# A delta-rule head's decay matrix kept in device memory between its two uses

## The chip, the cores and the metric

One Trainium2 chip, of which one core runs the kernel: a TensorE (PE, with its weight loads listed apart as PEld), a VectorE (DVE), a ScalarE (ACT), a GpSimd (POOL) and a SyncE (SP) that only issues transfers. The metric is the time of one launch on the device in microseconds, taken outside the profiler; it was 1414.25 us in the median of three runs (1413.27, 1414.25 and 1415.5). A profile is one further execution, with every instruction's start and duration.

## The reference

One layer of a hybrid block, for one sequence of 512 tokens and a model width of 1024, in 32-bit floats. The normed input is projected to twelve groups of columns. Branch A is a gated delta rule with 8 heads (keys and queries 128 wide, values 256 wide), branch B a retention with 4 heads; the two are gated, added, projected, and an MLP of width 4096 follows. For branch A the lines that matter here are these:

```python
decay = jnp.exp(jnp.where(causal, g_cum[..., :, None] - g_cum[..., None, :], -jnp.inf))
lower = jnp.where(strict, jnp.einsum('bhncd,bhnmd->bhncm', k_beta, k) * decay, 0.0)
t_inv = lax.linalg.triangular_solve(lower, eye, left_side=True, lower=True, unit_diagonal=True)
attn = jnp.where(causal, jnp.einsum('bhncd,bhnmd->bhncm', q, k) * decay, 0.0)
```

The matrix `decay` depends on the gates alone, is the same in both products, and is used twice for each head: once with the keys alone, to make the triangular matrix that is inverted, and once with queries and keys, to make the weights inside a chunk. The kernel works in chunks of 128 tokens, so a head has four such matrices of 128 by 128.

## The kernel before

The kernel is one program without loops at run time. A scheduler arranges it: each instruction goes to the queue of its engine in an order that the scheduler chooses from the order of the source, from priorities and from its own estimate of times, and each queue then runs strictly in that order. An instruction that waits holds up all behind it in its queue. Tiles with one tag share one buffer or a few (`bufs`): the next tile under the tag can be written only when every reader of the last one is done.

Most of the time goes into products with weights (lines 81 to 83: each product of exact halves is three matmuls of 512 columns). SP loads the weights in pieces of 512 KB, ACT rounds a piece to its high half (`whi`, L100) and DVE subtracts to get the low half (`wlo`, L101).

Branch A runs in this order of the source (lines 657 to 677): `keys(0)` for heads 0 to 3, `base_inverse(0)`, `values_queries(0)` for heads 0 and 1, `keys(1)` for heads 4 to 7, `double_blocks`, and then four rounds, each with the `recurrence` of two heads, the `values_queries` of the next two, the gating (`gated`) and a product with a branch weight. The parts overlap freely in time.

`decays(h, pool)` makes the four decay matrices of a head: for the two halves of the gate's logarithm, ACT scales a triangle of ones four times into `tg` (L390, eight instructions a head), PE multiplies each `tg` with a strict triangle into PSUM (L391, two matmuls a head) and ACT takes the exponential into `dt` (L393). It is called from `keys` (L438) and from `values_queries` (L555).

`dt` has one buffer, as the tag is given without `bufs`. In `keys`, eight DVE instructions read it for a head (L445 writes `mt`, which lives in `acc`; L448 scales `kd`), in `values_queries` four (L561 writes `at`, which POOL then masks at L565). `double_blocks` puts its own scratch `y` under the same tag (L505, written at L511 and L527, read by matmuls at L515, L518 and L530). So exponentials, these products and `y` take turns in one buffer.

POOL issues the transfers of the inverse through device memory from its own queue: `mt` out in four pieces (L458), back as one block to a partition (`mb`, L464), the finished inverses out (L481, L482) and back (`rt` L485, `rn` L495). Between them stand small memsets for the convolution (L357) and the mask (L565). The inverse itself is 31 steps of two DVE instructions (L473, L479). PSUM tiles under the tag `dl` have three banks, shared by decays, key products, inverses and recurrences.

Of the kernel before, what the change touches and what calls it, by code (L numbers as in the profile page):

```python
# [19 lines left out]
P = 128  # L20
# [40 lines left out]
def hybrid_block_kernel(ctx: ExitStack, tc: tile.TileContext, a: dict, out: bass.AP):  # L61
# [23 lines left out]
    def weights(src, k0, nk, c0, ncols, keep=None):  # L85
        """nk blocks of 128 rows, ncols columns, in exact halves; split ahead of other work that is due."""
        n = nk * ncols
        i = next(loads)
        raw = raw_pools[i % len(raw_pools)].tile([P, 1024], F32, tag="raw", name="raw", bufs=2)
        nc.sync.dma_start(  # L90
            raw[:, :n].rearrange("p (k c) -> p k c", k=nk),
            src[k0 * P : (k0 + nk) * P, c0 : c0 + ncols].rearrange("(k p) c -> p k c", p=P),
        )
        if keep is None:
            hi = ring.tile([P, 1024], F32R, tag="whi", name="whi")
            lo = ring.tile([P, 1024], F32R, tag="wlo", name="wlo")
        else:
            hi, lo = keep
        with tc.high_priority(200 if i >= 6 else 0):
            nc.scalar.copy(hi[:, :n], raw[:, :n])  # L100
            nc.vector.tensor_tensor(lo[:, :n], raw[:, :n], hi[:, :n], ALU.subtract)  # L101
        return (
            hi[:, :n].rearrange("p (k c) -> p k c", k=nk),
            lo[:, :n].rearrange("p (k c) -> p k c", k=nk),
        )

    def feature_major(src, xs, c0, ncols, kts, krow0=0):
        """[feature, token] products of ncols columns: PSUM tiles of 128 features."""
        nf = ncols // P
        pss = [psm.tile([P, xs[0].shape[2]], F32, tag="mm", name="mm") for _ in range(nf)]  # L110
        step = 1024 // ncols
        for k0 in range(0, kts, step):
            wh, wl = weights(src, krow0 + k0, step, c0, ncols)
            for f in range(nf):
                fs = slice(f * P, (f + 1) * P)
                for kk in range(step):
                    kt = k0 + kk
                    mm3(
                        pss[f],
                        (wh[:, kk, fs], wl[:, kk, fs]),  # L120
                        (xs[0][:, kt, :], xs[1][:, kt, :]),
                        kt == 0,
                        kt == kts - 1,
                    )
        return pss

    def token_major(src, lhs, c0, kts, krow0=0):
        """[token, 512 columns] products: one PSUM tile for each 128 tokens."""
        pss = [psm.tile([P, T], F32, tag="mm", name="mm") for _ in range(4)]
        for k0 in range(0, kts, 2):  # L130
            wh, wl = weights(src, krow0 + k0, 2, c0, 512)
            for t in range(4):
                tt = slice(t * P, (t + 1) * P)
                for kk in range(2):
                    kt = k0 + kk
                    mm3(
                        pss[t],
                        [x[:, tt] for x in lhs(kt)],
                        (wh[:, kk, :], wl[:, kk, :]),
                        kt == 0,  # L140
                        kt == kts - 1,
                    )
        return pss
# [4 lines left out]
    def rsqrt(xv, n, name):  # L148
        """1/sqrt of a positive [P, n] tile."""
        yi = sm.tile([P, n], I32, tag=f"rs_i{n}", name="rs_i")  # L150
# [13 lines left out]

# [1 line left out]
    cmat = cp.tile([P, 3 * P], F32, name="cmat")  # L166
# [13 lines left out]

# [1 line left out]
    xs = [act.tile([P, 8, T], F32R, tag="actT", name="actT") for _ in range(2)]  # L182
# [8 lines left out]
    def root(v):  # L191
        """1/sqrt of a positive [P, n] tile."""
        n = v.shape[1]
# [9 lines left out]
    def rows_to_features(xn, t, dst):  # L203
        """Transposes the [128 tokens, 1024] tile into the halves dst."""
        tt = slice(t * P, (t + 1) * P)
# [9 lines left out]
    with tc.tile_pool(name="xp", bufs=2) as xp:  # L215
# [62 lines left out]

# [1 line left out]
        baT = xp.tile([16, T], F32, tag="baT", name="baT")  # L280
# [44 lines left out]
    def gate_rows(pss, o_t, zt):  # L325
        """o * rstd * silu(z) in place, token-major."""
        for t in range(4):
# [25 lines left out]

# [1 line left out]
    def conv_silu(ps, ch, dst, pool):  # L355
# [28 lines left out]
    def decays(h, pool):  # L384
        """exp(sum of g over (m, c]) for m <= c, else 1: [m, chunk, c]."""
        pd = psx.tile([P, T], F32, tag="dl", name="dl", bufs=3)
# [5 lines left out]
        dt = pool.tile([P, 4, P], F32, tag="dt", name="dt")  # L392
        nc.scalar.activation(dt, pd.rearrange("p (c n) -> p c n", c=4), AF.Exp)  # L393
        return dt

# [9 lines left out]
    with tc.tile_pool(name="pa", bufs=1) as pa:  # L405
# [46 lines left out]
        def base_inverse(g4, pool):  # L452
            """Unit lower triangular inverses of 64 diagonal 32-blocks, one to a partition."""
            scr_m, scr_r, scr_t = (dr.tile([4, 16, 1024], F32, tag=f"scr{i}", name="scr") for i in range(3))
# [33 lines left out]
        def double_blocks(pool, scr_r, m0):  # L488
            """From 32-blocks to the transposed 128-block inverses, for two heads."""
            rn = pool.tile([P, 8, 64], F32, tag="qf", name="rn", bufs=2)  # L490
# [42 lines left out]
        def values_queries(g2, pool):  # L533
# [16 lines left out]
            for hh in range(2):  # L550
# [3 lines left out]
                sum_squares(to_tokens(qf[:, hh, :]), ssq[:, 4 * hh : 4 * hh + 4], junk)  # L554
                dt = decays(h, pool)  # L555
                pk = psx.tile([P, 4, P], F32, tag="dl", name="dl", bufs=3)
# [10 lines left out]
            )  # L567
            # r_q * dk**-0.5
            rq = pool.tile([P, 8], F32, tag="rq", name="rq", bufs=2)
# [4 lines left out]
        def recurrence(g2, vq, pool):  # L574
# [61 lines left out]

            # rstd of the true output r_q * dk**-0.5 * o; a half of it for silu(z)
            v = pool.tile([P, 8], F32, tag="ov", name="ov")
# [40 lines left out]

# [1 line left out]
    with tc.tile_pool(name="pb", bufs=1) as pb_:  # L681
# [129 lines left out]

# [1 line left out]
    with tc.tile_pool(name="pm", bufs=1) as pm:  # L813
# [10 lines left out]
        def row_tiles(src, lhs, krow0, keeps, done):  # L824
            """[token, 1024] products, two tiles of 128 tokens and then one by one; the weights stay on chip."""
            kept = {}
# [27 lines left out]
        def norm_halves(parts):  # L854
            """rstd of rows that come in two halves; what else is done with a half may follow it."""
            ss = sm.tile([P, 2], F32, tag="nh_s", name="nh_s")
# [9 lines left out]
        def add_normed(t, parts, w):  # L866
            """x2[t] += rmsnorm(parts) * w."""
            fw = pm.tile([P, D], F32, tag="ym", name="fw", bufs=2)
# [129 lines left out]
```

## Time and profile before

| | |
|---|---|
| three timed runs | 1413.27, 1414.25, 1415.5 us |
| span of the profiled execution, first to last instruction | 1410.7 us |
| the profiled execution's own time outside the profiler | not listed; the median run is 3.55 us above the span |
| PE busy | 1394.6 us, 99% |
| DVE busy | 809.0 us, 57% |
| ACT busy | 571.7 us, 41% |
| POOL busy | 53.0 us, 4% |
| device memory read and written | 124.93 MB and 3.67 MB |

Busy time is the union of an engine's instructions. PE's instructions overlap in the pipeline, so that a matmul of 512 columns is shown with 0.39 us and the next one starts 0.23 us after it; the chain of waits, which follows the last instruction back to what released it at each step, counts the latter. The granted clock of PE is 0.997 of full speed over the span. All that the change touches lies in the first 390 us.

### The profile page before, as it was taken

To read this page: it belongs to the slowest core of one execution; us is meant where nothing else is said; L and a number is where in the kernel's file an instruction comes from. 1 tells how busy PE (TensorE), PEld (TensorE's weight loads), DVE (VectorE), ACT (ScalarE), POOL (GpSimd) and SP (SyncE) were. 2 spreads that over 40 slices of the span, in tenths; PEclk is the share of its full clock that TensorE was granted. 3 is DMA by queue.
4 is the path that set the end of the run, shared out by engine and by line. 5 is a ranking of instruction groups with operands and counts; after the bars stand their busy time and mean duration, and the time that the engine had idled before them with its cause. 6 is when DMAs were issued, how large, how long until landed. Compare 5 with 4: busy or idle time off the path is not lost.

```text
span 1410.7 us, 17493 instructions
## 1 busy us (share of the span) xinstructions
PE 1394.6 (99%) x6766; PEld 1139.7 (81%) x6766; DVE 809.0 (57%) x1463; ACT 571.7 (41%) x1082; POOL 53.0 (4%) x100
## 2 busy tenths in 40 slices
PE   8999999999999999999999999999999999999997
PEld 6888787878888888888888888888888888888886
DVE  5599889944765564436445455445685333343445
ACT  6778564624534233233342323223464333132331
POOL 1111300200000000000000000000000000000000
PEclk9999999999999999999999999999999999999999
DMA  5232412221221342333223232232724232232321
GB/s 157 75 95 75 114 31 75 73 76 46 89 90 48 103 135 83 97 95 93 75 90 98 75 90 90 75 90 75 238 90 135 90 101 94 92 102 90 108 72 60
DMA packets 69942, 129.74 MB, mean 92 GB/s; under 512 B 4608, under 2 KB 18066, under 8 KB 69859
## 3 DMA queue, kind: packets, MB, share of 16 engines
q1 hardware_dynamic: 66128, 119.03, 26.8%
q0 software_dynamic: 3008, 8.34, 2.1%
q8 instruction: 53, 0.87, 0.3%
q10 hardware_dynamic: 722, 1.25, 0.2%
q14 instruction: 31, 0.25, 0.1%
HBM read 124.93 MB, written 3.67 MB: 91 GB/s over the span
## 4 chain that ended last, share of the span: by engine, by line
PE 92%; DVE 5%; ACT 1%; issue 1%; DMA 1%; SPq 0%; DVEq 0%; ACTq 0%
PE mm L81 27%; PE mm L82 27%; PE mm L83 27%; PE tr L179 2%; DVE c_y L367 1%; PE dl L83 1%; PE dl L82 1%; PE dl L81 1%; PE dl L598 1%; PE dl L626 1%; DVE wlo L101 1%; PE dl L590 1%; PE dl L606 1%; PE dl L619 1%; DVE tmp L473 1%
## 5 line engine op out<-in xcount | busy, mean ns | idle before, releaser
L101 DVE TENSOR_TENSOR wlo<-raw,whi 128x1024 fp32r<-128x1024 f32 x208 | 254.3, 1223 | 387.8 <-ACT whi L100 386.6
L100 ACT CAST whi<-raw 128x1024 fp32r<-128x1024 f32 x208 | 218.3, 1050 | 514.0 <-PE mm L82 282.1
L82 PE MATMUL mm<-actT,whi 128*128 128x512 f32 (+1 forms) x528 | 207.7, 393 | 1.2 <-DVE actT L213 1.2
L81 PE MATMUL mm<-actT,whi 128*128 128x512 f32 (+1 forms) x528 | 206.8, 393 | 1.0 <-ACT actT L212 1.0
L83 PE MATMUL mm<-actT,wlo 128*128 128x512 f32 (+1 forms) x528 | 207.3, 393 | 0.0
L81 PE MATMUL mm<-whi,actT 128*128 128x512 f32 x472 | 185.9, 394 | 0.1
L82 PE MATMUL mm<-wlo,actT 128*128 128x512 f32 x472 | 185.4, 393 | 0.0
L83 PE MATMUL mm<-whi,actT 128*128 128x512 f32 x472 | 185.2, 393 | 0.0
L81 PEld LDWEIGHTS mm<-actT,whi 128*128 128x128 f32 x528 | 99.8, 189 | 21.4 <-ACT actT L212 1.3
L82 PEld LDWEIGHTS mm<-actT,whi 128*128 128x128 f32 x528 | 100.1, 190 | 20.4 <-DVE actT L213 1.4
L83 PEld LDWEIGHTS mm<-actT,wlo 128*128 128x128 f32 x528 | 100.0, 189 | 19.0
L81 PE MATMUL mm<-hn,whi 128*128 128x512 f32 (+1 forms) x288 | 106.3, 370 | 0.6 <-DVE r L921 0.5
L82 PE MATMUL mm<-hn,whi 128*128 128x512 f32 (+1 forms) x288 | 106.2, 369 | 0.0
L83 PE MATMUL mm<-hn,wlo 128*128 128x512 f32 (+1 forms) x288 | 106.0, 369 | 0.0
L81 PEld LDWEIGHTS mm<-whi,actT 128*128 128x128 f32 x472 | 88.6, 188 | 19.0 <-ACT c_y L365 0.5
L83 PEld LDWEIGHTS mm<-whi,actT 128*128 128x128 f32 x472 | 88.6, 188 | 18.2
L82 PEld LDWEIGHTS mm<-wlo,actT 128*128 128x128 f32 x472 | 88.6, 188 | 17.9
L81 PE MATMUL mm<-og,whi 128*128 128x512 f32 x256 | 100.3, 392 | 0.0
L82 PE MATMUL mm<-og,whi 128*128 128x512 f32 x256 | 99.6, 389 | 0.0
L83 PE MATMUL mm<-og,wlo 128*128 128x512 f32 x256 | 98.5, 390 | 0.0
L367 DVE SCALAR_TENSOR_TENSOR c_y<-c_raw,convw,c_y 128x512 f32<-128x512 f32 x96 | 70.5, 752 | 3.4 <-ACT c_y L365 2.8
L81 PEld LDWEIGHTS mm<-hn,whi 128*128 128x128 f32 x288 | 54.0, 187 | 11.4 <-issue 0.7
(286 smaller groups left out, 2077.0 us busy)
## 6 DMA issues: line engine op xcount, KB each, us to landing
raw<-in_w_in_dram SPq DMA_DIRECT2D x113, 512.0 KB, 3.6
raw<-in_w_up_dram SPq DMA_DIRECT2D x36, 512.0 KB, 3.6
raw<-in_w_down_dram SPq DMA_DIRECT2D x32, 512.0 KB, 3.6
raw<-in_w_br_a_dram SPq DMA_DIRECT2D x16, 512.0 KB, 3.6
raw<-in_w_br_b_dram SPq DMA_DIRECT2D x16, 512.0 KB, 3.6
raw<-in_w_out_dram SPq DMA_DIRECT2D x8, 512.0 KB, 3.7
x<-in_x_dram SPq DMA_DIRECT2D x4, 512.0 KB, 6.4
acc<-in_x_dram POOLq DMA_DIRECT2D x4, 512.0 KB, 3.8
```

The lines of the kernel that those rows point to most:

```text
L81: nc.tensor.matmul(ps, lh, rh, start=first, stop=False)
L82: nc.tensor.matmul(ps, lh, rl, start=False, stop=False)
L83: nc.tensor.matmul(ps, ll, rh, start=False, stop=last)
L100: nc.scalar.copy(hi[:, :n], raw[:, :n])
L101: nc.vector.tensor_tensor(lo[:, :n], raw[:, :n], hi[:, :n], ALU.subtract)
L179: nc.tensor.transpose(ps, src, ident)
L367: nc.vector.scalar_tensor_tensor(y, raw[:, j : j + T], tap(j), y, ALU.mult, ALU.add)
L473: nc.vector.tensor_tensor(t3, mb3[:, j, j + 1 : 32].unsqueeze(2).to_broadcast([64, nr, ni]), rb3[:, j, 0:ni].unsqueeze(1).to_broadcast([64 ...
L590: nc.tensor.matmul(ks[:, hh, :], kf[:, h0 + hh, cs], state[:, hh, :], start=True, stop=True)
L598: nc.tensor.matmul(px[:, hh, :], rt[:, nn[hh], :], vx[:, hh, :], start=True, stop=True)
L606: nc.tensor.matmul(pc[:, hh, :], kd[:, nn[hh], :], vn[:, hh, :], start=True, stop=True)
L619: nc.tensor.matmul(qs[:, hh, :], qf[:, hh, cs], prev[:, hh, :], start=True, stop=True)
```

## The change

`decays`, which is now called from `keys` alone, also writes its result to device memory, to a tile of its own for each head, by a transfer that POOL issues. `values_queries` no longer computes the matrices: `decays_again` takes the same kind of tile under the same tag `dt` and fills it by a transfer from device memory, again issued by POOL. What is left out of the diff below is the removal of comments and docstrings.

```diff
     def decays(h, pool):
...
         dt = pool.tile([P, 4, P], F32, tag="dt", name="dt")
         nc.scalar.activation(dt, pd.rearrange("p (c n) -> p c n", c=4), AF.Exp)
+        kept_decays[h] = dr.tile([P, 4, P], F32, tag=f"dt{h}", name="dts", bufs=1)
+        nc.gpsimd.dma_start(kept_decays[h], dt)
+        return dt
+
+    kept_decays = {}
+
+    def decays_again(h, pool):
+        dt = pool.tile([P, 4, P], F32, tag="dt", name="dt")
+        nc.gpsimd.dma_start(dt, kept_decays[h])
         return dt
...
-                dt = decays(h, pool)
+                dt = decays_again(h, pool)
```

## Rows read from the trace of the kernel before

**Rows 1.** Page, block 4: the chain that ended last, by engine.

```profile
PE 92%; DVE 5%; ACT 1%; issue 1%; DMA 1%; SPq 0%; DVEq 0%; ACTq 0%
```

**Rows 2.** Stretches: length, busy of PE, PEld, DVE, ACT, POOL, clock, DMA.

```profile
90.00:147.50 57.50, 56.34 (x278) 45.91 (x276) 56.93 (x146) 43.59 (x122) 8.86 (x12) 1.00 0.28 83
...
205.50:251.00 45.50, 45.29 (x213) 36.35 (x212) 44.81 (x110) 24.63 (x45) 4.65 (x6) 1.00 0.20 60
262.00:290.00 28.00, 27.90 (x237) 22.70 (x235) 19.74 (x58) 16.76 (x54) 5.80 (x11) 1.00 0.21 65
```

**Rows 3.** DVE's waits from 89.5 to 147.5: total us, times, longest.

```profile
DVE c_y L367 <- ACT c_y L365: 0.5, 1, 0.5
DVE wlo L101 <- ACT whi L100: 0.2, 1, 0.2
```

**Rows 4.** DVE's waits from 205.5 to 251.

```profile
DVE at L561 <- PE dl L559: 0.3, 1, 0.3
```

**Rows 5.** PE's weight loads' waits from 118 to 260.

```profile
PEld tr L179 <- DVE c_y L371: 1.0, 1, 1.0
```

**Rows 6.** Chain of waits, decay matmuls for queries: start us, us, what.

```profile
91.17 0.47 PE dl L391 x2
...
204.02 0.67 PE dl L391 x2
...
385.55 0.47 PE dl L391 x2
```

**Rows 7.** Groups by line: busy us, mean ns, idle before.

```profile
L390 ACT ACTIVATE tg<-cmat,ghi 128x128 fp32r<-128x128 f32 x64 | 22.3, 401 | 4.5 <-PE dl L391 3.2 <-DVE ghi L315 1.2
```

**Rows 8.** POOL's transfers of 256 KB from 40 to 450: count, KB, us to landing.

```profile
scr<-mrb POOLq DMA_DIRECT2D x2, 256.0 KB, 2.9
...
scr<-acc POOLq DMA_DIRECT2D x2, 256.0 KB, 3.5
...
mrb<-scr POOLq DMA_DIRECT2D x1, 256.0 KB, 3.3
acc<-scr POOLq DMA_DIRECT2D x1, 256.0 KB, 4.0
```

**Rows 9.** Timeline of ACT, `dt` of heads 5, 6, 7: start us, us.

```profile
149.98 0.60 ACT L393 ACTIVATE dt<-dl 128x512 f32<-128x512 f32 x1 [0.99 <-DVE kd L448]
...
154.06 0.59 ACT L393 ACTIVATE dt<-dl 128x512 f32<-128x512 f32 x1
...
157.57 0.60 ACT L393 ACTIVATE dt<-dl 128x512 f32<-128x512 f32 x1 [0.59 <-DVE kd L448]
```

**Rows 10.** Timeline of POOL at the same time.

```profile
149.56 2.57 POOL L485 DMA_DIRECT2D rt<-scr  x4 [0.43 <-DMA scr<-mrb]
```

**Rows 11.** Timeline of DVE, the next writer of that buffer.

```profile
161.55 0.88 DVE L511 COPY y<-dl 32x256 f32<-32x256 f32 x2
```

**Rows 12.** Timeline of DVE, first products of heads 2 and 3.

```profile
205.69 0.35 DVE L561 SCALAR_TENSOR_TENSOR at<-dl,rk,dt 128x128 f32<-128x128 f32 x1 [0.34 <-PE dl L559]
...
208.65 0.34 DVE L561 SCALAR_TENSOR_TENSOR at<-dl,rk,dt 128x128 f32<-128x128 f32 x1
```

**Rows 13.** Timeline of POOL, the first inverse's way through memory.

```profile
81.12 2.62 POOL L458 DMA_DIRECT2D scr<-acc  x4 [19.59 <-DVE kd L448]
...
88.69 0.55 POOL L464 DMA_DIRECT2D mrb<-scr  x1 [0.53 <-issue]
```

**Rows 14.** Timeline of DVE, first step of that inverse.

```profile
93.71 0.18 DVE L473 TENSOR_TENSOR tmp<-mrb 64x31 f32<-64x31 f32 x1
```

**Rows 15.** Timeline of DVE, products of heads 4 and 5.

```profile
271.50 1.13 DVE L561 SCALAR_TENSOR_TENSOR at<-dl,rk,dt 128x128 f32<-128x128 f32 x4 [0.60 <-PE dl L559]
...
277.12 1.13 DVE L561 SCALAR_TENSOR_TENSOR at<-dl,rk,dt 128x128 f32<-128x128 f32 x4 [0.30 <-ACT dt L393]
```

**Rows 16.** Timeline of POOL, the same store of 256 KB in both inverses.

```profile
144.61 0.55 POOL L481 DMA_DIRECT2D scr<-mrb  x1 [8.75 <-DVE rs_t L156]
...
249.07 1.15 POOL L481 DMA_DIRECT2D scr<-acc  x1 [3.62 <-DVE acc L479]
```

## The prediction

> **What bounds the kernel now.** I read the page first: busy times and the chain of waits. PE is busy for 99% of the span (the table above) and the chain runs through PE for 92% and through DVE for 5% [rows 1]. The reader should take from it that PE time removed can be worth its full length, but that about 70 us of the chain belong to DVE, and that one has to know where. All that is removed lies before 390 us, so the second view is the table of stretches. From 90 to 147.5 us DVE is busy for 56.93 of 57.50 us, and from 205.5 to 251 us for 44.81 of 45.50; from 262 to 290 it is busy for only 19.74 of 28 while PE is full [rows 2]. The list of DVE's waits says the same: two waits of 0.5 and 0.2 us in the first stretch [rows 3], 0.3 us in the second for anything that matters here [rows 4]. At the end of the first stretch PE waits 1.0 us for a DVE instruction of the convolution [rows 5]. So PE and DVE run neck and neck in two stretches, with DVE setting the pace there, and PE alone sets it afterwards. The chain of waits for the decay matmuls of the queries (first, fourth and last of the six pairs that stand as pairs) shows what each costs PE: 0.47 us a head [rows 6]; the 0.67 at 204.02 has 0.20 of other waiting in it. Two heads (3 and 5) have their two matmuls apart; I count them at 0.47 too.
>
> **What goes.** For eight heads: two matmuls, eight scalings on ACT and one exponential. On PE that is 8 x 0.47 = 3.76 us. On ACT it is 8 x (8 x 0.40 + 0.59) = 30 us of instruction time [rows 7, 9], but ACT is busy for only 43.59 of 57.50 us in its fullest of these stretches [rows 2] and off the chain, so I cost it at nothing; if ACT were what holds DVE's splits, at most the 0.2 us of that wait [rows 3] is to be had.
>
> What of the 3.76 us reaches the end is settled by stretch. Heads 0 and 1 (0.94 us) lie from 91 to 105 us, inside the first DVE stretch. DVE has no less to do than before; it can run earlier only by the time it idles after 91 us, 0.2 us; the 0.5 us wait comes before [rows 3]. Bounds 0 and 0.94; I take 0.2. Heads 2 and 3 (0.94 us) stand at the head of the second DVE stretch. DVE idles 0.3 us for the product that follows the matmuls of head 2 [rows 4, 12], which an earlier product would give back, but see the load below: I take 0. Heads 4 to 7 (4 x 0.47 = 1.88 us) lie where PE alone is full [rows 2]: 1.88. Sum: 2.1 us gained.
>
> **What comes: eight stores.** A transfer of 256 KB issued by POOL lands 2.9 to 4.0 us after its issue [rows 8]; for stores 2.9 to 3.5, and I use 3.2. The store reads `dt`, so the next writer of that one buffer now waits for the landing and not only for DVE's eight reads. In `keys(1)`: the matrix of head 5 is there at 149.98 + 0.60 = 150.58 [rows 9]. POOL is then in the middle of four issues of 0.64 us for `rt` [rows 10]; between two of them the store goes out at about 151.0 and lands at 154.2, when the exponential of head 6 started at 154.06: 0.15 late. Then 154.8 + 3.2 = 158.0 against 157.57 for head 7, 0.45 late, and 158.6 + 3.2 = 161.8 against the `y` of `double_blocks` at 161.55 [rows 11], 0.3 late. I take 0.4 us, all of it on PE, whose inverse matmuls read `y`. The low bound is 0 (issue at once, 2.9 us: 153.5, 157.6, 161.1). The high bound has the store behind all four `rt` issues and 3.5 us: 152.1 + 3.5 = 155.6, then 159.7, then 163.8, 2.3 us late. Queued behind a waiting store on POOL are the rest of the `rt` issues and the third `rn`; their readers come after `y` and lose nothing more than it does.
>
> In `keys(0)` the same spacing holds, and heads 2 and 3 could be late by up to the same 2.3 us. That delays the four pieces of `mt` that POOL sends out at 81.12. Their last issue ends at 83.74, and they are fetched back at 88.69 [rows 13]; DVE first uses them at 93.71 [rows 14]. The fetch takes 3.3 us [rows 8], so 1.7 us are spare behind it, and before it 5 us, of which a landing takes at most 4. I cost this at nothing; without that cover it would be up to 2.3 us into a stretch where DVE has none to give.
>
> **Eight loads.** Each waits for the last reader of the buffer; I use the 3.3 us of the load [rows 8]. Head 0's buffer is free at 81.1, when DVE's last read for head 3 lets POOL go on [rows 13], ten us before its use. Head 2's is held by `y` until the matmuls before 204.02 [rows 6] are done: 204.0 + 3.3 = 207.3 against 205.69, 1.6 late. DVE's four products take some 1.4 us among other work, so head 3's load goes out at 208.7 and lands at 212.0 against 208.65 [rows 12], 3.4 late. What is queued behind on DVE is the second inverse, 62 instructions of which two thirds are still to come, and the splits of the weights for PE. The bounds are 0, if the order puts these instructions ahead of the products, and 3.4, if DVE stands. I take 0: among DVE's waits in both stretches no transfer occurs [rows 3, 4], although the inverse's blocks come by transfers of the same size, so the order has been leaving room for them. Head 5's load goes out when head 4's products end at 272.63 and lands at 275.9, before 277.12 [rows 15]: 0. Heads 1 and 7 are late or early by less than 2 us with much other work before their reader: 0. Also, the matmuls of the next parts find a `dl` bank free more often, as the decays took one each; I give it nothing.
>
> The Trainium skill has a rule against this change: by "SBUF — State Buffer", section "SBUF: two separate sides", POOL cannot write the descriptors of its transfers while DVE runs a copy in one of its fast modes. The trace agrees in one place: the same store takes POOL 0.55 us at 144.61 and 1.15 us at 249.07 [rows 16]. By the row at 144.61 an issue costs what the sum has; by the rule each one beside DVE costs up to 0.6 us more. It has a rival below.
>
> **The sum.** 2.1 - 0.4 = 1.7 us gained. The profiled span of 1410.7 becomes 1409.0. Its own time outside the profiler isn't listed; the median run lies 3.55 us above the span, and I let that stand: 1414.25 - 1.7 = 1412.5 us.
>
> **Rivals.**
> 1. PE gets it all: 1414.25 - 3.76 = 1410.5 us. For it speaks the 92% of PE in the chain [rows 1], and that the order of every queue is chosen anew, so that DVE's full stretches may be filled otherwise. Against it: DVE's work there is unchanged.
> 2. The one `dt` buffer becomes the bound, and the kernel gets slower. Each store and each load holds it for more than 3 us, in `keys(1)` up to 2.3 us are lost and in the second DVE stretch 3.4: 1414.25 - 2.1 + 2.3 + 3.4 = 1417.9 us. It decides from the point at which these waits pass 2.1 us together. For it: DVE and PE are both nearly without idle time there [rows 2], so a stall isn't absorbed. Against it: no DVE wait on a transfer stands in these stretches.
> 3. POOL's issue is stretched beside DVE. Five transfers follow one another through the buffer with somebody waiting (stores of heads 5, 6, 7, loads of 2 and 3); at 1.15 - 0.55 = 0.6 us each that is 3.0 us: 1412.5 + 3.0 = 1415.5 us. Against it: only one issue in the trace is stretched like this [rows 16]. The skill's section above would have this case.
> 4. Nothing: the 1.88 us of the last heads too are given back at the next wait for ACT or DVE, 1414.3 us. For it: the gating and the recurrence that follow alternate between the engines. Against it: PE was full there.
>
> **Chances.** The forecast 0.38, with a range of its own from 1411.2 to 1414.0 (bounds 0 to 2.3 us of store wait cut to the likelier half); rival 1 0.22; rival 2 0.24; rival 3 0.08; rival 4 0.08. The range from 1409.8 to 1418.0 leaves out some 0.1 on the side of rival 2 and a little less on that of rival 1. A measurement of this kernel can tell a change from none from about 0.2%, 2.8 us: faster is below 1411.4, slower above 1417.1. Faster gets rival 1 and 0.05 of the forecast, 0.27; slower gets 0.20 of rival 2 and 0.02 of rival 3, 0.22; the rest is 0.51.
>
> **What would show it.** PE's instructions fall by 16 and its busy time by some 4 us. In the chain the DVE share before 251 us stays or grows. The exponentials of heads 6 and 7 name a transfer as what they waited for, by less than 0.5 us. DVE's waits name `dt` for heads 2 and 3, and if that is over 1 us in sum, rival 2 has begun. POOL's issues of the new transfers last 0.55 to 0.65 us; 1 us or more speaks for rival 3. PE's waits from 262 to 392 us stay as they are; if they grow by over 1 us, rival 4. I am wrong altogether if the new order of the queues moves PE's waits elsewhere by more than these sums, which shows as lost time after 400 us.

## The result, and the profile after

The changed kernel took 1420.38 us in the median of six executions against 1413.47 for the kernel before on the same chip: ratio 1.004 (95% interval 1.0029 to 1.0051), so 0.4% slower. Forecast were 1412.5 and a range up to 1418.0. Five of the six lie from 1416.89 to 1421.79 and enter the ratio; the sixth, which is the one that was profiled, had a mean granted clock of 0.754 and a span of 1729.2 us, so everything below is read from another profile of the same kernel, the first experiment, at 0.996. That set took 1418.79 us, ratio 1.0029 (1.0017 to 1.0041).

The line numbers of the changed kernel: stores L395, loads L402, key products L451, `mt` L454, `kd` L457, the inverse L482 and L488, the values' scaling L549, the queries' products L570. First its page: the span, PE, the new transfers with their median landing, and the chain by engine.

```profile
span 1416.5 us, 17422 instructions
...
PE 1393.0 (98%) x6750; PEld 1137.7 (80%) x6750; DVE 807.8 (57%) x1463; ACT 550.3 (39%) x1010; POOL 64.1 (5%) x116
...
PE 88%; DVE 5%; DMA 3%; ACT 2%; issue 1%; POOL 1%; SPq 0%; DVEq 0%; ACTq 0%; POOLq 0%
...
dts<-dt POOLq DMA_DIRECT2D x8, 256.0 KB, 3.2
```

The median landing is the 3.2 us that the prediction took. But in the chain PE has lost 4 points against [rows 1], and transfers and ACT have gained 3. The chain between 71 and 83 us says where: in `keys(0)` it runs exponential, store, exponential, store.

```profile
71.68 0.60 ACT dt L393
...
72.56 4.94 DMA dts<-dt
...
77.61 0.61 ACT dt L393
...
78.50 3.47 DMA dts<-dt
...
82.07 0.61 ACT dt L393
```

The same exponentials on ACT's timeline (start, duration, in brackets the idle time before it and who ended it); in the kernel before none of them waited for a transfer:

```profile
71.68 0.59 ACT L393 ACTIVATE dt<-dl 128x512 f32<-128x512 f32 x1
...
77.61 0.60 ACT L393 ACTIVATE dt<-dl 128x512 f32<-128x512 f32 x1 [2.54 <-DMA dts<-dt]
...
82.07 0.60 ACT L393 ACTIVATE dt<-dl 128x512 f32<-128x512 f32 x1 [1.06 <-DMA dts<-dt]
...
156.45 0.60 ACT L393 ACTIVATE dt<-dl 128x512 f32<-128x512 f32 x1 [1.72 <-DMA dts<-dt]
```

ACT's own idle time would cost nothing by itself. But the key products of the same head need a bank of PSUM under the tag `dl`. In PE's queue the decay matmuls of the next head stand ahead of these products (at 74.89), and the bank that the products take is the one that the exponential of their own head empties, so they wait for it. PE's queue is in order, so the weight products behind them wait too. PE's timeline:

```profile
75.59 0.39 PE L81 MATMUL mm<-actT,whi 128*128 128x512 f32 x1
78.26 0.94 PE L451 MATMUL dl<-kf 128*128 128x128 f32 x6 [2.29 <-ACT dt L393]
```

The first matmul starts at 75.59 and its successor should follow 0.23 us later; it follows at 78.26. That is the largest single loss, 2.4 us.

The waits of the whole stretch from 40 to 300 us, first ACT's, then PE's weight loads, then DVE's (total us, times, longest):

```profile
ACT dt L393 <- DMA dts<-dt: 5.3, 3, 2.5
```

```profile
PEld dl L451 <- ACT dt L393: 3.8, 2, 2.7
...
PEld mm L82 <- DVE wlo L101: 1.9, 1, 1.9
PEld mm L81 <- ACT c_y L365: 1.8, 6, 0.5
PEld dl L391 <- DVE acc L454: 1.4, 1, 1.4
```

```profile
DVE at L570 <- DMA dt<-dts: 1.4, 2, 0.8
```

The second line of PE's list is a loss that nothing in the prediction speaks of. The chain at that place, inside the second inverse:

```profile
254.77 0.45 PE tr L179 x4
...
255.25 0.69 DVE vt L549
...
256.09 0.66 DVE c_y L367
...
256.88 1.15 DVE wlo L101
...
258.07 0.64 PE mm L82
258.71 0.43 PE mm L83
```

PE transposes, DVE scales the result and has more of the convolution and the inverse queued, and only then splits the weights that PE needs. After it PE's matmuls follow one another by 0.43 us instead of 0.23. The stretches show why; columns as in [rows 2], and the seventh figure is the granted clock.

```profile
254.00:258.00 4.00, 2.40 (x12) 1.45 (x10) 3.96 (x10) 1.91 (x3) 0.10 (x1) 1.00 0.00 0
258.00:262.00 4.00, 3.93 (x12) 3.21 (x13) 4.00 (x9) 1.70 (x4) 0.65 (x2) 0.57 0.65 183
```

In the kernel before the same times are full, at full clock:

```profile
254.00:258.00 4.00, 4.00 (x20) 3.23 (x19) 3.94 (x8) 1.82 (x6) 2.72 (x5) 1.00 0.33 66
258.00:262.00 4.00, 4.00 (x20) 3.02 (x20) 3.78 (x6) 2.37 (x8) 0.00 (x0) 1.00 0.40 131
```

A granted clock of 0.57 over 4 us is mostly the lower of the two levels, 1.2 GHz. On PE's timeline the next seven large matmuls and four transposes start within 3.74 us, from 258.07 to 261.81; at 0.23 us a matmul and 0.45 for the four transposes it would be 2.06. So some 1.7 us are lost to the clock, after a stall of 1.9.

### The profile page after: what moved, and what is told of

Same layout as the page of the kernel before. It is cut to its first block, busy times and chain, and to the rows that moved or that the text cites. A ratio compares the mean times of both kernels' runs of the same rounds, so it can differ in the third digit from the quotient of the medians.

```text
span 1729.2 us, 17422 instructions
## 1 busy us (share of the span) xinstructions
PE 1715.0 (99%) x6750; PEld 1228.1 (71%) x6750; DVE 814.9 (47%) x1463; ACT 552.8 (32%) x1010; POOL 60.7 (4%) x116
## 4 chain that ended last, share of the span: by engine, by line
PE 98%; DMA 0%; DVE 0%; ACT 0%; SPq 0%; issue 0%; DVEq 0%; ACTq 0%
PE mm L82 29%; PE mm L83 29%; PE mm L81 28%; PE tr L179 2%; PE dl L607 1%; PE dl L635 1%; PE dl L81 1%; PE dl L82 1%; PE dl L83 1%; PE dl L628 1%; PE dl L599 1%; PE dl L615 1%; PE dl L568 1%; PE dl L451 1%; DMA x<-in_x_dram 0%; PE dl L539 0%
## 5 line engine op out<-in xcount | busy, mean ns | idle before, releaser
L82 PE MATMUL mm<-actT,whi 128*128 128x512 f32 (+1 forms) x528 | 244.9, 464 | 1.1 <-DVE actT L213 1.1
L81 PE MATMUL mm<-actT,whi 128*128 128x512 f32 (+1 forms) x528 | 240.2, 456 | 0.5 <-ACT actT L212 0.5
L83 PE MATMUL mm<-actT,wlo 128*128 128x512 f32 (+1 forms) x528 | 240.3, 456 | 0.0
L82 PE MATMUL mm<-wlo,actT 128*128 128x512 f32 x472 | 216.6, 459 | 1.5 <-DVE wlo L101 1.5
L83 PE MATMUL mm<-whi,actT 128*128 128x512 f32 x472 | 218.1, 462 | 0.0
L81 PE MATMUL mm<-whi,actT 128*128 128x512 f32 x472 | 217.3, 461 | 0.0
L81 PEld LDWEIGHTS mm<-actT,whi 128*128 128x128 f32 x528 | 107.8, 204 | 41.8 <-ACT actT L212 0.9
L82 PEld LDWEIGHTS mm<-actT,whi 128*128 128x128 f32 x528 | 104.7, 198 | 41.3 <-DVE actT L213 1.3
L82 PE MATMUL mm<-hn,whi 128*128 128x512 f32 (+1 forms) x288 | 122.5, 425 | 0.0
L81 PE MATMUL mm<-hn,whi 128*128 128x512 f32 (+1 forms) x288 | 122.3, 425 | 0.1
L81 PEld LDWEIGHTS mm<-whi,actT 128*128 128x128 f32 x472 | 94.6, 200 | 39.0 <-ACT c_y L365 0.6
L83 PE MATMUL mm<-hn,wlo 128*128 128x512 f32 (+1 forms) x288 | 122.3, 426 | 0.0
L83 PEld LDWEIGHTS mm<-whi,actT 128*128 128x128 f32 x472 | 93.3, 198 | 38.4
L81 PE MATMUL mm<-og,whi 128*128 128x512 f32 x256 | 117.1, 458 | 0.0
L83 PE MATMUL mm<-og,wlo 128*128 128x512 f32 x256 | 116.0, 459 | 0.0
L82 PE MATMUL mm<-og,whi 128*128 128x512 f32 x256 | 115.7, 452 | 0.0
```

What stands on the lines that cost most here:

```text
L81: nc.tensor.matmul(ps, lh, rh, start=first, stop=False)
L82: nc.tensor.matmul(ps, lh, rl, start=False, stop=False)
L83: nc.tensor.matmul(ps, ll, rh, start=False, stop=last)
```

## The experiments

The theory after these rows: a store reads the only buffer of `dt` until it has landed, the next exponential waits, and PE stands behind it (the hold). Its rivals: the loads cost it, by the same buffer; the transfers cost it by their traffic; it is the new order of the queues; or PE is granted a lower clock. Differences are given to the kernel before in the same set (1414.14 in the first four runs, 1414.45 in the next four, then 1413.87 and 1413.95), with the interval of the ratio behind; by these a difference is known to some 1.4 us (2.4 for the stores alone). The ratio is not that of the medians, so that near zero the two can differ in sign.

**Both halves apart.** The changed kernel as it is; the queries' decays left out altogether; stores without loads; loads without stores.

> The changed kernel as it is, for an undisturbed profile. Theory A (the one buffer dt is held by transfers): 1416 to 1421 us; waits of ACT and DVE for the new transfers, direct or through the buffer, add up to 4 us or more before 260 us, and PE loses that much there. Theory B (the queues were put into another order and the transfers are innocent): the same time, waits for transfers under 1.5 us in all, and PE's lost time stands at places that have nothing to do with dt. Theory C (TensorE is granted a lower clock, 0.991 to 0.995 of full speed in four of the changed kernel's five timed runs, where the profile of before shows 0.997): the time follows the granted clock from run to run, some 1415 us at 0.998 and 1419 at 0.992.

Only the removal:

```diff
-        kept_decays[h] = dr.tile([P, 4, P], F32, tag=f"dt{h}", name="dts", bufs=1)
-        nc.gpsimd.dma_start(kept_decays[h], dt)
...
-                dt = decays_again(h, pool)
...
-                        ..., rk[:, 4 * h + c : 4 * h + c + 1], dt[:, c, :],
+                        ..., rk[:, 4 * h + c : 4 * h + c + 1], ones,
```

> The queries' decay matrices are left out altogether: neither computed, stored nor loaded, a tile of ones stands in their place (so the decay is missing from the weights inside a chunk). This is the gain alone. Theory A: faster than before by the 2 to 3.8 us of the prediction, 1409.7 to 1411.5 us. Theory B: no fixed amount; if the new order alone costs, it is not faster than before, 1413 to 1420 us. Theory C: if the clock falls because PE has gaps, it stays near 0.997 here and the time near 1410.

Only the stores, with the queries computing again:

```diff
-        nc.gpsimd.dma_start(kept_decays[h], dt)
+        if keep:
+            ...
+            nc.gpsimd.dma_start(kept_decays[h], dt)
...
-                dt = decays_again(h, pool)
+                dt = decays(h, pool, keep=False)
```

> The stores alone: the keys' matrices are written to device memory as in the changed kernel, but the queries compute theirs again as before. Theory A: slower than before by the store's part, 0.4 (the prediction's step) to 4 us, with exponentials waiting for stores. Theory B: within 1 us of before or any amount, without waits for transfers to explain it. Theory C: same as before if the clock is 0.997.

Only the loads, from an input that is there from the start:

```diff
-        nc.gpsimd.dma_start(kept_decays[h], dt)
...
-        nc.gpsimd.dma_start(dt, kept_decays[h])
+        nc.gpsimd.dma_start(dt, a["c_decay"][h % 4].rearrange("p (c n) -> p c n", c=4))
```

> The loads alone: no stores; the queries load 256 KB a head under the tag dt, as in the changed kernel, but from a constant of branch B that lies in device memory from the start (so the decay inside a chunk has wrong values). Theory A: between the removal alone and the changed kernel: the removal's time plus up to 3.4 us for heads 2 and 3, 1411 to 1415 us. If the stores are what costs, it equals the removal alone within 1 us. Theory B: no relation to the removal alone. Theory C: the time follows the granted clock.

| kernel | us | difference | ratio |
|---|---|---|---|
| changed, as it is | 1418.79 | +4.65 | 1.0029 (1.0017 to 1.0041) |
| removal alone | 1409.02 | -5.12 | 0.9965 (0.9954 to 0.9977) |
| stores alone | 1428.34 | +14.20 | 1.0101 (1.0084 to 1.0118) |
| loads alone | 1410.84 | -3.30 | 0.9976 (0.9965 to 0.9987) |

The loads aren't it: with them alone the kernel gains 3.3 us. The stores alone cost 14.2 us, more than the changed kernel loses beyond the removal (9.8). Their exponentials on ACT's timeline wait as above:

```profile
76.68 0.60 ACT L393 ACTIVATE dt<-dl 128x512 f32<-128x512 f32 x1 [2.74 <-DMA dts<-dt]
...
81.16 0.60 ACT L393 ACTIVATE dt<-dl 128x512 f32<-128x512 f32 x1 [1.08 <-DMA dts<-dt]
```

and the stretch around 258 is worse: PE is busy for 1.55 and 2.92 of 4 us, and the clock is at the lower level for all of the second.

```profile
254.00:258.00 4.00, 1.55 (x9) 0.87 (x7) 4.00 (x11) 1.90 (x3) 0.10 (x1) 0.90 0.02 4
258.00:262.00 4.00, 2.92 (x7) 1.95 (x8) 3.55 (x6) 1.36 (x3) 1.21 (x3) 0.50 0.46 103
```

The clock has a part in this. All four runs of the stores alone have a granted clock of 0.991 to 0.993, where the kernel before has 0.994 to 0.999. In the profile the clock is 0.90, 0.50 and 0.75 in the three stretches of 4 us from 254 to 266 and 0.72 from 300 to 306: some 10 us at the lower level, which cost up to 5 us (an estimate from these figures). The changed kernel's loss isn't the clock alone: its six runs have 0.996 to 0.998, and the one at 0.998 took 1416.45 us, where five runs of the kernel before at 0.998 took 1413.07 to 1415.55. In the set of the result its five runs go with the clock, from 1416.89 us at 0.998 to 1421.79 at 0.992.

**Is it the hold or the transfer?** A store of the same size, by the same queue, that reads `kf` instead of `dt`: as many bytes move, and the buffer is free at once.

```diff
-        nc.gpsimd.dma_start(kept_decays[h], dt)
+        nc.gpsimd.dma_start(kept_decays[h], kf[:, h, :].rearrange("p (c n) -> p c n", c=4))
```

> The changed kernel, but each store sends out the head's keys (kf, 256 KB, never written again in this part) in place of dt, and the queries load that back (so the decay inside a chunk has wrong values). The same transfers are issued at the same places on the same queue; only the hold on the buffer dt is gone. Theory A (the store's hold on dt makes the next exponential wait, and PE with it): the time of the loads alone, 1408 to 1412.5 us, and no exponential waits for a store. Theory D (the transfers themselves cost: POOL's issues, traffic beside the weights): the changed kernel's time, 1416.5 to 1420. Theory B (the new order of the queues): near the changed kernel's time, or anything without relation to the hold.

> The stores alone (queries compute their matrices again), the store again sending kf in place of dt. Theory A: what the stores alone cost (14 us over before) is gone nearly whole: 1412 to 1417 us. Theory D: it stays, 1424 to 1430 us. Theory B: no relation; a new order may cost or not.

Measured: the changed kernel with it 1412.44 (-2.0; 0.9982, 0.9973 to 0.9992), the stores alone with it 1414.31 (-0.1; 1.0001, 0.9991 to 1.001). Without the hold eight stores cost nothing that can be measured, and the changed kernel is 6.7 us faster (4.65 + 2.0). PE at the place of the largest loss, in the changed kernel without the hold:

```profile
76.95 0.40 PE L81 MATMUL mm<-actT,whi 128*128 128x512 f32 x1
77.18 1.05 PE L451 MATMUL dl<-kf 128*128 128x128 f32 x8
77.99 0.48 PE L82 MATMUL mm<-actT,whi 128*128 128x512 f32 x1
```

The key products follow 0.23 us after the matmul before them. So the hold is the cause, and eight stores as such are not. The traffic doesn't stay in its place, though: a store of `kf` needn't wait for the exponential, and those of heads 1 to 3 go out at 54.92, 60.79 and 63.20 us instead of 72.56, 78.50 and 82.97. What the same traffic costs at the later times is answered by the common pool of buffers below. And of the 6.7 us the order may still have a part, as the scheduler knows of the hold and arranges the queues around it.

**Waiting or order?** The hold for one half of the heads only (`dt` stored for these, `kf` for the others).

```diff
-        nc.gpsimd.dma_start(kept_decays[h], dt)
+        nc.gpsimd.dma_start(kept_decays[h], dt if h < 4 else kf[:, h, :].rearrange(...))
```

> The changed kernel with dt stored for heads 0 to 3 and kf (no hold) sent in its place for heads 4 to 7 (whose decay inside a chunk has then wrong values). Theory A: heads 0 to 3 cost the waits of keys(0), 2.5 us that PE stood in the changed kernel at 76 us, perhaps also the stall at 256 us if that comes from keys(0) being late: 1414 to 1417 us. Theory B: no relation to the two kernels it lies between (1412.4 and 1418.8).

The other kernel has `h >= 4`.

> The other half: dt stored for heads 4 to 7, kf for heads 0 to 3 (wrong values there). Theory A: the waits of keys(1), 1.9 us of PE between 150 and 157 us, and the stall at 256 us if it comes from there: 1414 to 1418 us; the two halves' costs over 1412.4 add up to some 6.4 us. Theory B: no relation, the halves don't add up.

Measured: held for heads 0 to 3, 1414.13 (+0.2; 0.9999, 0.9989 to 1.0009); for heads 4 to 7, 1415.14 (+1.2; 1.001, 1.0 to 1.0019). Set against the kernel without any hold (-2.0), heads 0 to 3 cost 2.2 us and heads 4 to 7 cost 3.2. The first kernel has on PE, DVE, ACT and SP exactly the order of the one without hold, so its 2.2 us aren't a new order on these four, and PE's timeline has them in one piece, ended by the exponential:

```profile
79.67 0.60 PE L451 MATMUL dl<-kf 128*128 128x128 f32 x3 [2.52 <-ACT dt L393]
```

The second one has exactly the order of the changed kernel on those four engines, which has another line of the kernel at 832 of the 6750 places of PE's queue and 255 of the 1463 of DVE's than the order without hold. The hold of heads 4 to 7 therefore acts twice: as a wait, of 1.0 us on PE, and by the order that the scheduler chooses around it.

```profile
PEld dl L451 <- ACT dt L393: 1.0, 1, 1.0
```

The loss before 258 us belongs to that order, since it is here as well, while with a hold of heads 0 to 3 alone PE is full there. First held for heads 4 to 7, then for heads 0 to 3:

```profile
254.00:258.00 4.00, 2.33 (x11) 1.63 (x11) 4.00 (x11) 1.43 (x3) 0.10 (x1) 1.00 0.13 18
258.00:262.00 4.00, 4.00 (x18) 3.04 (x17) 4.00 (x6) 2.46 (x4) 1.09 (x2) 1.00 0.95 271
```

```profile
254.00:258.00 4.00, 3.95 (x19) 3.36 (x20) 3.97 (x7) 2.36 (x7) 1.33 (x3) 1.00 0.37 96
```

The clock stays up after that same stall, 1.00 against 0.57. So the sum of the whole hold: 2.2 + 3.2 = 5.4 us of 6.7. The remaining 1.3 lie within the noise of these differences; that they are the 1.7 us which the lower clock level took in the one profile of the changed kernel, where both holds meet, isn't shown.

**Other ways to free the buffer.** No run here has two buffers for `dt`, or `y` in a tile of its own. One run has one tag for `tg`, `dt` and `y` together with three buffers, as many as the two tags had before:

```diff
-            tg = pool.tile([P, 4, P], F32R, tag="tg", name="tg", bufs=2)
+            tg = pool.tile([P, 4, P], F32R, tag="tg", name="tg", bufs=3)
...
-        dt = pool.tile([P, 4, P], F32, tag="dt", name="dt")
+        dt = pool.tile([P, 4, P], F32, tag="tg", name="dt", bufs=3)
```

(and `y` and the tile of `decays_again` likewise.)

> The changed kernel with one tag of three buffers for tg (which had two), dt and y (which had one together), so that a store or load holds one of three. It computes the whole reference. Theory A: 1408.5 to 1413 us, faster than before, with exponentials that wait little for stores. Theory D: 1416 to 1420. Theory B: any.

The second one has the stores issued by ACT, straight behind the exponential, with the buffers as they are:

```diff
-        nc.gpsimd.dma_start(kept_decays[h], dt)
+        nc.scalar.dma_start(kept_decays[h], dt)
```

> The changed kernel with the stores issued by ACT, right behind the exponential, in place of POOL; the hold on dt stays, but it ends sooner if what made the stores land 3.5 to 4.9 us after their issue was POOL's way of issuing. Theory A: shorter waits, by some 1 to 2 us for each of four exponentials, 1411 to 1417 us; if the landing stays as long, no gain. Theory D: POOL's part of the cost goes, the traffic's stays. Theory B: no relation.

Measured: 1413.89 for the common pool (-0.6; 0.9996, 0.9986 to 1.0005) and 1415.23 for ACT's stores (+0.8; 1.0008, 0.9999 to 1.0018). Both are faster than the changed kernel, neither beats the one before. With the common pool no exponential waits for a transfer any more, although the stores of heads 1 to 3 go out at 65.63, 72.76 and 79.28 us, near the times of the changed kernel. This kernel is 1.45 us above the one with `kf`, which is within the noise, so traffic near those times isn't what costs the 6.7 us; for heads 4 to 7 the times differ by up to 26 us, and that part isn't separated. An earlier issue shortens the hold only in part (two exponentials still wait 1.95 and 1.38 us for a store). The common pool in the kernel before, as a control:

> The kernel before, with the one tag of three buffers for tg, dt and y: the control for the changed kernel with that pool. Theory A: it takes no transfer away, so the time is that of before within 2 us, 1412.5 to 1416.5. If it is faster by 3 us or more, the pool is worth something by itself and the pooled changed kernel (1413.9 us) shows a loss against it; if slower by that much, the pool costs by itself and hides a gain.

1414.10 (+0.2; 0.9996, 0.9986 to 1.0005): the pool by itself is worth nothing.

**More of it.** Common pool and ACT's stores together; then the matrices of heads 0 to 3 kept on the chip in a buffer that stands empty until the gating (`og`), those of heads 4 to 7 stored from the other such buffer, so that no store holds `dt`; and the same with ACT's stores. The edit of the second:

```diff
-        dt = pool.tile([P, 4, P], F32, tag="dt", name="dt")
+        if h % 4 == 0:
+            made.append(act.tile([P, 4, T], F32, tag="og", name="dk"))
+        dt = made[h // 4][:, h % 4, :].rearrange("p (c n) -> p c n", c=4)
...
-        nc.gpsimd.dma_start(kept_decays[h], dt)
+        if h >= 4:
+            ...
+            nc.gpsimd.dma_start(kept_decays[h], dt)
...
+        if h < 4:
+            return made[0][:, h, :].rearrange("p (c n) -> p c n", c=4)
```

> The changed kernel with the pool of three buffers and the stores issued by ACT. Theory A: both ways of shortening the hold together, 1409 to 1414 us. What the pooled kernel lost against the loads alone (3.1 us: 1413.9 against 1410.8) comes back if it was the rest of the hold; it stays if it is the new order of the queues (Theory B) or the stores' traffic (Theory D).

> No hold at all, and the whole reference: the matrices of heads 0 to 3 stay on chip, in one of the two buffers of 8 KB a partition that the gated features (og) use only later, without store or load; those of heads 4 to 7 are written into the other and stored from there, so no exponential waits for a store, and are loaded under dt after 220 us. Theory A: as the loads alone or the removal alone, 1408.5 to 1412 us, faster than before and than the changed kernel. Theory B: no relation; 1412 to 1420 us. Theory D: near the changed kernel without hold, 1412.4 us, less what four stores and four loads fewer give.

> The same with the four stores issued by ACT. Theory A: without a hold the issuing engine doesn't matter: within 1.5 us of the kernel with POOL's stores. Theory D: faster by what POOL's issues cost there.

Measured: 1416.19 (+2.3; 1.0014, 1.0004 to 1.0024), 1416.13 (+2.3; 1.0016, 1.0007 to 1.0026) and 1421.79 (+7.9; 1.0057, 1.0041 to 1.0072). All three are slower than before, though in none does an exponential wait for a store. In the first, a hold is still there, one step earlier: the scalings `tg` that feed an exponential take a buffer of the same pool.

```profile
ACT tg L390 <- DMA dts<-dt: 3.9, 1, 3.9
```

The last one's losses lie in other places: its weight products wait for DVE, and from 150 to 165 us the clock is 0.69. Its waits of PE's weight loads from 85 to 170 us, and that stretch:

```profile
PEld mm L83 <- DVE wlo L101: 5.8, 2, 2.9
PEld tr L179 <- ACT tg L390: 1.6, 1, 1.6
```

```profile
150.00:165.00 15.00, 12.48 (x109) 9.14 (x109) 9.88 (x24) 3.40 (x5) 4.50 (x8) 0.69 0.42 115
```

The last two differ only in who issues four stores that nobody waits for, and lie 5.7 us apart, with another line at 667 of the 6750 places of PE's queue: the order of the queues, together with the clock, which differs too (0.990 to 0.995 in the four runs of the last kernel, 0.994 to 0.999 in the ten of the other), can be worth as much here as the whole change. Which part of the order it is, I can't say. In all three, ACT runs the exponentials of heads 5 and 6 early (126 to 139 us; 150 and 153 without the hold, in one buffer), and I took that for the cause; but the last kernel below has them at 125.63 and 135.86 and loses nothing there, so the early exponentials alone aren't it.

**Half of it.** Heads 0 to 3 compute twice, as before, and only heads 4 to 7 are stored and loaded; without and with the common pool.

```diff
-                dt = decays_again(h, pool)
+                dt = decays(h, pool, keep=False) if h < 4 else decays_again(h, pool)
...
-        nc.gpsimd.dma_start(kept_decays[h], dt)
+        if keep and h >= 4:
+            ...
+            nc.gpsimd.dma_start(kept_decays[h], dt)
```

> The whole reference: heads 0 to 3 compute their matrices twice as in the kernel before, heads 4 to 7 store and load as in the changed kernel. Theory A: keeps the 1.9 us of heads 4 to 7, pays keys(1)'s hold, 1412 to 1416 us. Theory B: any, 1411 to 1420.

> The same with the pool of three buffers. Theory A: the hold of keys(1) gone, 1411 to 1413.5 us, faster than before if the order of the queues does not take it back. Theory B: any, 1411 to 1420.

Measured: 1413.52 (-0.4; 1.0003, 0.9992 to 1.0014) and 1411.30 (-2.65; 0.9982, 0.9973 to 0.9992). The second one, which does all of the work, beats both kernels, by 0.18% against the one before. Its page, and what its exponentials waited for from 40 to 300 us: PE, no transfer.

```profile
span 1410.2 us, 17443 instructions
...
PE 90%; DVE 6%; ACT 2%; DMA 1%; issue 1%; SPq 0%; POOL 0%; DVEq 0%; ACTq 0%
```

```profile
ACT dt L393 <- PE dl L391: 4.1, 3, 2.5
```

## Why the prediction was wrong

The four runs and the store that holds nothing make one column of terms, each the difference to the kernel before it in the list:

| term | forecast | measured |
|---|---|---|
| the queries' decays go | -2.1 | -5.1 (removal alone) |
| loads come | 0 | +1.8 (loads alone less that) |
| stores come, without the hold | 0 | +1.3 (no hold, less loads alone) |
| the buffer is held by the stores | +0.4 | +6.7 (changed, less no hold) |
| sum | -1.7 | +4.65 |

Each measured term below the first is a difference of two, known to some 2 us: the middle two could be nothing, the hold could not, and the interval of the first (3.3 to 6.5) leaves out the 2.1.

**The step that failed is the price of the stores' hold on `dt`**, 0.4 us for 6.7, and in it first the store in `keys(0)`: "I cost this at nothing; without that cover it would be up to 2.3 us". The delay was of the forecast size, 2.29 us of PE's idle time in the trace and 2.2 us between the runs that differ in the hold of heads 0 to 3 alone. The cover was the wrong one. I followed the late heads to the inverse that they feed, found 1.7 and 5 us spare there, and stopped. The nearer reader was PE itself: the exponential frees a `dl` bank, the key products of the same head come next in PE's queue, and behind them stood weight products without any other reason to wait. The question for a delayed instruction is who is next in each queue that touches its tiles, its PSUM bank included, and not only where its result is used at last.

**The second part of that step**: the landing. 3.2 us was taken, from [rows 8], and 3.2 is the median; the first store of `keys(0)` that somebody waited for took 4.94. At 72.63 us, 0.07 after it, SP issued two weight pieces of 512 KB. The bounds of 2.9 to 3.5 came from four stores, and I didn't look at what else was being moved beside them. That the weights stretched it isn't shown.

**`keys(1)`**: 0.4 forecast, bounds 0 to 2.3. Heads 4 to 7 cost 3.2 us, beyond the bound. One exponential waits 1.72 us for a store, where under 0.5 was forecast, and again PE stands behind its bank (1.1 us), not behind `y` as forecast; but the stall of 1.9 us before 258, a hundred microseconds later, comes by the order that the scheduler made of the hold, and in the profile of the changed kernel 1.7 us of lower clock follow it. The prediction named a new order as what would make it wrong altogether, gave it no chance of its own, and looked for it after 400 us; it came at 254.

**The removal** was mis-sized the other way: 5.1 us for 2.1. PE's instructions fell by 16 as forecast (6766 to 6750); its busy time fell by 1.6 us in the changed kernel and by 7.7 with the removal alone, where some 4 were forecast. The whole 3.76 us of PE time fits, the 2.1 doesn't. So DVE's full stretches [rows 2] didn't bind: DVE is as full with the removal alone (59.16 us of the 60 from 90 to 150, and 59.43 before), and the kernel is faster. That the scheduler filled them otherwise, as rival 1 said, fits this and isn't shown further. A stretch in which an engine is busy for 99% is only a bound if its work can't be done at another time.

**The loads**: 0 forecast, and the feared 3.4 us of heads 2 and 3 didn't come. DVE's waits for loads are 1.4 us in two (above): 0.76 for head 2, none for head 3, and 0.67 for head 5. So heads 2 and 3 stay under the mark of 1 us that was set for rival 2. After 300 us head 7 comes, where less than 2 us was said:

```profile
397.92 1.13 DVE L570 SCALAR_TENSOR_TENSOR at<-dl,rk,dt 128x128 f32<-128x128 f32 x4 [3.22 <-DMA dt<-dts]
```

PE runs on through it without a gap, so it costs nothing there. Rival 2's mechanism, the one buffer that becomes the bound, did decide the case, but its place was the stores and PE, not the loads and DVE. That its 1417.9 us lies near the measured 1418.8 is luck, as 3.4 of it are the loads of heads 2 and 3.

**POOL's issue** was not stretched: the new stores take 0.56 and 0.59 us in the places where somebody waits.

```profile
72.56 0.56 POOL L395 DMA_DIRECT2D dts<-dt  x1 [10.86 <-ACT dt L393]
...
152.70 0.59 POOL L395 DMA_DIRECT2D dts<-dt  x1 [1.38 <-ACT dt L393]
```

Rival 3 fell: all 16 new issues take 0.54 to 0.60 us. The inverse's own store has a longer issue again, and beside it DVE copies from SBUF to SBUF:

```profile
149.37 1.11 DVE L489 COPY mrb<-mrb 64x1024 f32<-64x1024 f32 x1
```

```profile
149.48 1.12 POOL L490 DMA_DIRECT2D scr<-mrb  x1 [12.03 <-DVE acc L454]
```

With this the Trainium skill's rule on the shared port ("SBUF — State Buffer", section "SBUF: two separate sides") agrees as far as the trace tells (it doesn't tell the copy's mode): no such copy runs beside any of the 16 new issues, so the rule's case, as the prediction gave it, didn't arise there.

## What to carry to other kernels

A transfer out of a tile is a reader of it until it lands, so storing from a tile with one buffer turns each store into a wait for the next writer; before such a change, count the buffers, not the bytes. Follow each delayed instruction to the next one in every queue that shares a tile or a bank with it, because an in-order engine passes the delay on long before the result is needed. Where a scheduler arranges the queues, a store that only delays can also change an order far away, so a change whose gain is 4 us of 1414 needs a run and not a sum.

## What the runs showed of the hardware

The landing of a store of 256 KB in the changed kernel's profile went from 2.3 us (at 82.97, the transfer engines 0.29 busy from 83 to 85.3) to 4.94 (at 72.56, 0.66 busy), with the median at 3.2. The busy share alone doesn't order them: the store at 152.70 landed in 3.65 us with the engines 0.83 busy.

POOL took 1.12 us to issue a store where DVE had begun a copy 0.11 us before, and 0.54 to 0.60 us for the 16 new transfers, beside which DVE did other work.

PE's clock fell to its lower level after one stall of 1.9 us (0.57 from 258 to 262 us) and stayed at 1.00 after a stall of the same length at the same place in the run that held heads 4 to 7 alone. What tells the two apart stays open.
